# Average pooling 2x2x2: eight loads of 16 to 48 KB rows through one ring, and a store held back by an added wait

## The chip, the cores and the metric

One core of a Trainium2 chip. The metric is the device time of one execution in microseconds (us), lower is better. All runs told of here are fast (the full clock was granted). Times quoted are medians. A ratio is the mean time of one kernel's fast runs over that of the kernel before's fast runs of the same rounds, so it is not quite the ratio of the two medians.

## The reference, cut to what matters

```python
# x: (8, 32, 32, 32, 32) float32, kernel_size = 2; result: (8, 32, 16, 16, 16)
window = x[:, :, 2*i:2*i+2, 2*j:2*j+2, 2*k:2*k+2]
result[:, :, i, j, k] = np.mean(window, axis=(-3, -2, -1))
```

33.55 MB are read and 4.19 MB written, with seven additions and one product per result: a kernel about moving data. The 256 pairs of batch and channel lie on the 128 partitions in two halves (`t` = 0 and 1), each with rows of 128 KB. A "32 KB row" below is the piece of such a row that a load brings to each partition; its result is one eighth of it.

## The kernel before

```python
KF = 256                                    # 256 floats: 1 KB of a row
pool_in = ctx.enter_context(tc.tile_pool(name="pin", bufs=5))      # five buffers of 32 KB per partition
obuf = [pool_out.tile([P, 16 * KF], F32, name=f"obuf{t}") for t in range(2)]

plan = [(0, 0, (32,)), (0, 32, (32,)), (0, 64, (32,)), (0, 96, (32,)),
        (1, 0, (32,)), (1, 32, (32,)), (1, 64, (16, 16)), (1, 96, (16, 16))]

def pool_unit(buf, t, k0, kb):              # three Vector steps, in place in the loaded buffer
    nc.vector.tensor_add(out=b..., in0=a[:, :, 0], in1=a[:, :, 1])          # depth
    nc.vector.tensor_add(out=c, in0=bv[:, :, 0], in1=bv[:, :, 1])           # width
    nc.vector.tensor_tensor_reduce(out=obuf[t]..., scale=0.125, ...)        # height, times 1/8

for t, k0, parts in plan:
    tin = pool_in.tile([P, 32 * KF], F32, tag="tin", name="tin")
    ...                                     # one load per part on the Sync queue, then pool_unit on each

for t, k0, kb in [(1, 0, 12), (0, 0, 16), (1, 12, 4)]:    # three stores, on the same queue
    nc.sync.dma_start(out=ov[...], in_=obuf[t][:, k0 * KF:(k0 + kb) * KF])
# ... (after compiling: the first load is moved ahead of the opening barrier, and the
#      waits for the stores to the very end)
```

All transfers are issued by the Sync engine. It issues in program order, so a store that must wait for the Vector engine holds up everything behind it: in the run "the wait raised by four counts" below, the results of the 12 KB store were ready at 78.3 us, but it was issued at 82.89, right after the held 16 KB store.

Of the kernel before, what the change touches and what calls it, by code (L numbers as in the profile page):

```python
# [1 line left out]

# [4 lines left out]

F32 = mybir.dt.float32
KF = 256


@with_exitstack
def pool_rows(
    ctx: ExitStack,
    tc: tile.TileContext,
    x: bass.AP,
    kernel_size: int,
    out: bass.AP,
):
    nc = tc.nc  # L20
    assert kernel_size == 2, "only kernel_size == 2 supported"

    B, C, D, H, W = x.shape
    P = nc.NUM_PARTITIONS
    assert (B * C, D, H, W) == (2 * P, 32, 32, 32)
    add = mybir.AluOpType.add



    xv = x.rearrange("b c d h w -> (b c) (d h w)")  # L30
    ov = out.rearrange("b c d h w -> (b c) (d h w)")




    pool_in = ctx.enter_context(tc.tile_pool(name="pin", bufs=5))
    pool_out = ctx.enter_context(tc.tile_pool(name="pout", bufs=1))
    obuf = [pool_out.tile([P, 16 * KF], F32, name=f"obuf{t}") for t in range(2)]
    dummy = pool_out.tile([P, 1], F32, name="dummy")


    plan = [
        (0, 0, (32,)),
        (0, 32, (32,)),
        (0, 64, (32,)),
        (0, 96, (32,)),
        (1, 0, (32,)),
        (1, 32, (32,)),
        (1, 64, (16, 16)),
        (1, 96, (16, 16)),  # L50
    ]

    def pool_unit(buf, t, k0, kb):

        od = kb // 8
        a = buf.rearrange("p (o dd e) -> p o dd e", o=od, dd=2)
        b = buf[:, :od * 1024]
        nc.vector.tensor_add(  # L58
            out=b.rearrange("p (o e) -> p o e", o=od), in0=a[:, :, 0], in1=a[:, :, 1])
        bv = b.rearrange("p (e ww) -> p e ww", ww=2)  # L60
        c = buf[:, od * 1024:od * 1536]
        nc.vector.tensor_add(out=c, in0=bv[:, :, 0], in1=bv[:, :, 1])  # L62
        cv = c.rearrange("p (j hh k) -> p j hh k", hh=2, k=16)
        o0 = k0 * KF // 8
        nc.vector.tensor_tensor_reduce(  # L65
            out=obuf[t][:, o0:o0 + od * 256].rearrange("p (j k) -> p j k", k=16),
            in0=cv[:, :, 0], in1=cv[:, :, 1],
            scale=0.125, scalar=0.0, op0=add, op1=add, accum_out=dummy[:, :],
        )

    for t, k0, parts in plan:
        tin = pool_in.tile([P, 32 * KF], F32, tag="tin", name="tin")
        views = []
        o = 0
        for kb in parts:
            v = tin[:, o * KF:(o + kb) * KF]
            nc.sync.dma_start(
                out=v, in_=xv[t * P:(t + 1) * P, (k0 + o) * KF:(k0 + o + kb) * KF])
            views.append((v, k0 + o, kb))
            o += kb  # L80
        for v, k, kb in views:
            pool_unit(v, t, k, kb)



    for t, k0, kb in [(1, 0, 12), (0, 0, 16), (1, 12, 4)]:
        nc.sync.dma_start(
            out=ov[t * P:(t + 1) * P, k0 * KF:(k0 + kb) * KF],
            in_=obuf[t][:, k0 * KF:(k0 + kb) * KF],
        )  # L90


def kernel(tc: tile.TileContext, x: bass.AP, kernel_size: int, out: bass.AP):
    nc = tc.nc
    pool_rows(tc, x, kernel_size, out)
    tc.close()
    tc.compile()  # L97
    blocks = nc.main_func.blocks



    opening, program = blocks[0].instructions, blocks[tc.starting_block_idx].instructions
    load = next(i for i in program if isinstance(i, mybir.InstDMACopy))
    assert load.engine == nc.sync.engine
    barrier = next(
        n for n, i in enumerate(opening)
        if i.engine == load.engine and isinstance(i, mybir.InstDrain))
    program.remove(load)
    opening.insert(barrier, load)




    closing = blocks[-1].instructions
    stores = [
        i for i in program
        if isinstance(i, mybir.InstDMACopy) and "out_" in i.outs[0].memref]
    kept = [u.id for i in stores for u in i.sync_info.on_update]
    final = next(
        i for i in closing  # L120
        if i.engine == nc.sync.engine and isinstance(i, mybir.InstDrain))
    waits = {w.id: w for w in final.sync_info.on_wait}
    closing[closing.index(final)] = mybir.InstDrain(
        name=final.name, engine=final.engine, ins=[], outs=[], is_reset_sema=False,
        sync_info=mybir.SyncInfo(
            on_wait=[w for n, w in waits.items() if n not in kept], on_update=[]))


    reset = next(
        n for n, i in enumerate(closing)  # L130
        if isinstance(i, mybir.InstDrain) and i.is_reset_sema)
    first, stop = closing[reset].reset_range_start, closing[reset].reset_range_stop
    assert isinstance(closing[reset + 1], mybir.InstISA)
    while len(closing) > reset:
        closing.pop()
    n = first
    while n < stop:
        m = n
        while m < stop and m not in kept:
            m += 1  # L140
        if m > n:
            closing.append(mybir.InstDrain(
                name=nc.get_next_instruction_name(), engine=nc.gpsimd.engine, ins=[], outs=[],
                is_reset_sema=True, reset_range_start=n, reset_range_stop=m))
            nc.gpsimd.sem_clear(range(n, m))
        n = m + 1
    for n in kept:
        w = waits[n]
        closing.append(mybir.InstEventSemaphore(
            name=nc.get_next_instruction_name(), engine=nc.sync.engine, ins=[], outs=[],  # L150
            sync_info=mybir.SyncInfo(
                on_wait=[w],
                on_update=[mybir.SyncUpdate(
                    sync_type="semaphore", id=n, ant_name=w.ant_name,
                    update_mode="sem-sub-imm", update_value=w.wait_value)])))


# [1 line left out]
_INS = ['x', 'kernel_size']  # L159
_OUTS = [((8, 32, 16, 16, 16), 'float32')]  # L160

_NUMBERS = {'kernel_size': 2}


# [26 lines left out]
```

## Time and profile before

| | kernel before |
|---|---|
| time, first three runs | 91.36 us (91.27 to 91.69) |
| span of the profiled execution (instructions only) | 86.3 us |
| Vector engine busy | 64.0 us |
| last completion of a store by the packet records | 89.45 us |
| loads, stores | 10 (six of 32 KB rows, four of 16 KB rows), 3 |

The span ends with the last instruction, not with the last byte: here the stores go on for 3 us beyond it. So the span isn't the time. A "unit" is the Vector work on one load; the eight or ten units are counted from 1. A load or store is "completed" when its last packet is done; the page counts it as landed some 0.4 us later (the last store before: 85.14 + 4.7 = 89.8 us, last packet at 89.45). On a profile page each engine has a row of 40 digits, one for each fortieth of the span: the digit is the busy share in tenths (9 is 90% or more). Besides the page and its views, the text uses the trace's records of single DMA packets. One packet is one row of one partition; each of 16 engines carries 8 rows of a transfer and then a small completion packet. "Completion on the slowest engine" is the last of the 16.

### The profile page before, as it was taken

To read this page: it belongs to the slowest core of one execution; us is meant where nothing else is said; L and a number is where in the kernel's file an instruction comes from. 1 tells how busy PE (TensorE), PEld (TensorE's weight loads), DVE (VectorE), ACT (ScalarE), POOL (GpSimd) and SP (SyncE) were. 2 spreads that over 40 slices of the span, in tenths; PEclk is the share of its full clock that TensorE was granted. 3 is DMA by queue.
4 is the path that set the end of the run, shared out by engine and by line. 5 is a ranking of instruction groups with operands and counts; after the bars stand their busy time and mean duration, and the time that the engine had idled before them with its cause. 6 is when DMAs were issued, how large, how long until landed. Compare 5 with 4: busy or idle time off the path is not lost.

```text
span 86.3 us, 89 instructions
## 1 busy us (share of the span) xinstructions
DVE 64.0 (74%) x40; POOL 0.2 (0%) x4
## 2 busy tenths in 40 slices
DVE  0000049992999749992999749992999999999994
POOL 0000000000000000000000000000000000000000
DMA  8989997999969998899979998899999999999999
GB/s 243 395 380 441 486 486 334 395 486 486 486 289 441 486 486 380 349 486 486 486 304 425 486 486 380 365 471 387 463 387 463 387 463 395 456 425 412 433 431 441
DMA packets 1674, 36.60 MB, mean 424 GB/s; under 512 B 176, under 2 KB 176, under 8 KB 176
## 3 DMA queue, kind: packets, MB, share of 16 engines
q1 hardware_dynamic: 1674, 36.60, 99.4%
HBM read 33.55 MB, written 4.19 MB: 438 GB/s over the span
## 4 chain that ended last, share of the span: by engine, by line
DMA 61%; DVE 37%; issue 0%; DVEq 0%
DMA tin<-in_x_dram 61%; DVE tin L58 21%; DVE tin L62 11%; DVE obuf L65 6%; DVE dummy L65 0%; DVEq L97 0%
## 5 line engine op out<-in xcount | busy, mean ns | idle before, releaser
L58 DVE TENSOR_TENSOR tin<-tin 128x4096 f32<-128x4096 f32 (+1 forms) x10 | 35.7, 3569 | 20.5 <-DMA tin<-in_x_dram 20.5
L62 DVE TENSOR_TENSOR tin<-tin 128x2048 f32<-128x2048 f32 (+1 forms) x10 | 18.6, 1865 | 0.3
L65 DVE CUSTOM_DVE_ANT_1 obuf<-tin 128x1024 f32<-128x1024 f32 (+1 forms) x10 | 10.1, 1011 | 0.3
L65 DVE DVE_READ_ACCUMULATOR2_ANT dummy<- 128x1 f32 x10 | 0.8, 82 | 0.0
L172 POOL MEMSET const-bfloat16-1.0<- 128x1 bf16 x1 | 0.1, 102 | 0.0
L172 POOL MEMSET const-uint8-127<- 128x1 uint8 x1 | 0.1, 101 | 0.0
L172 POOL MEMSET const-float32-0.0<- 128x1 f32 x1 | 0.1, 99 | 0.2 <-issue 0.2
L172 POOL MEMSET const-float32-1.0<- 128x1 f32 x1 | 0.1, 98 | 0.0
## 6 DMA issues: line engine op xcount, KB each, us to landing
tin<-in_x_dram SPq DMA_DIRECT2D x6, 4096.0 KB, 34.8
tin<-in_x_dram SPq DMA_DIRECT2D x4, 2048.0 KB, 38.0
out_dram<-obuf SPq DMA_DIRECT2D x1, 2048.0 KB, 11.5
out_dram<-obuf SPq DMA_DIRECT2D x1, 1536.0 KB, 7.0
out_dram<-obuf SPq DMA_DIRECT2D x1, 512.0 KB, 4.7
```

The source lines that it names most:

```text
L58: nc.vector.tensor_add(out=b.rearrange("p (o e) -> p o e", o=od), in0=a[:, :, 0], in1=a[:, :, 1])
L62: nc.vector.tensor_add(out=c, in0=bv[:, :, 0], in1=bv[:, :, 1])
L65: nc.vector.tensor_tensor_reduce(out=obuf[t][:, o0:o0 + od * 256].rearrange("p (j k) -> p j k", k=16), in0=cv[:, :, 0], in1=cv[:, :, 1], s ...
L172: nc = _bacc.Bacc("TRN2", target_bir_lowering=False, num_devices=1)
```

## The change

The intent: the same 160 KB of buffer as one ring, cut so that fewer and longer loads fit; and a store of finished results first, held back until shortly before the other store is ready.

```diff
-    pool_in = ctx.enter_context(tc.tile_pool(name="pin", bufs=5))
+    ring = pool.tile([P, 160 * KF], F32, name="ring")
-    plan = [(0, 0, (32,)), (0, 32, (32,)), (0, 64, (32,)), (0, 96, (32,)),
-            (1, 0, (32,)), (1, 32, (32,)), (1, 64, (16, 16)), (1, 96, (16, 16))]
+    plan = [        # half, start, KB, place in the ring
+        (0, 0, 32, 0), (0, 32, 48, 32), (0, 80, 48, 80), (1, 0, 32, 128),
+        (1, 32, 32, 0), (1, 64, 32, 32), (1, 96, 16, 64), (1, 112, 16, 80)]
+        tc.keep_in_program_order(first)             # the first add of each unit
-    for t, k0, kb in [(1, 0, 12), (0, 0, 16), (1, 12, 4)]:
+    for t, k0, kb in [(0, 0, 16), (1, 0, 12), (1, 12, 4)]:
+    # the first store waits for the Vector counter that the second needs, less one
+    (n, store), (_, second) = stores[:2]
+    need, = [w for w in second.sync_info.on_wait if w.ant_name.startswith("DVE")]
+            w = copy.replace(w, wait_value=need.wait_value - 1)
+    program[n] = copy.replace(store, sync_info=mybir.SyncInfo(on_wait=waits, ...))
 ... (cut)
```

More of the change, by code (lines that the diff above doesn't have):

```diff
@@ L1 @@
+import copy
 from contextlib import ExitStack
@@ L31, in pool_rows @@
     ov = out.rearrange("b c d h w -> (b c) (d h w)")
-    pool_in = ctx.enter_context(tc.tile_pool(name="pin", bufs=5))
-    pool_out = ctx.enter_context(tc.tile_pool(name="pout", bufs=1))
-    obuf = [pool_out.tile([P, 16 * KF], F32, name=f"obuf{t}") for t in range(2)]
-    dummy = pool_out.tile([P, 1], F32, name="dummy")
+    pool = ctx.enter_context(tc.tile_pool(name="ring", bufs=1))
+    ring = pool.tile([P, 160 * KF], F32, name="ring")
+    obuf = [pool.tile([P, 16 * KF], F32, name=f"obuf{t}") for t in range(2)]
+    dummy = pool.tile([P, 1], F32, name="dummy")
     plan = [
-        (0, 0, (32,)),
-        (0, 32, (32,)),
-        (0, 64, (32,)),
-        (0, 96, (32,)),
-        (1, 0, (32,)),
-        (1, 32, (32,)),
-        (1, 64, (16, 16)),
-        (1, 96, (16, 16)),
+        (0, 0, 32, 0),
+        (0, 32, 48, 32),
+        (0, 80, 48, 80),
+        (1, 0, 32, 128),
+        (1, 32, 32, 0),
+        (1, 64, 32, 32),
+        (1, 96, 16, 64),
+        (1, 112, 16, 80),
     ]
@@ L57, in pool_unit @@
         b = buf[:, :od * 1024]
-        nc.vector.tensor_add(
+        first = nc.vector.tensor_add(
             out=b.rearrange("p (o e) -> p o e", o=od), in0=a[:, :, 0], in1=a[:, :, 1])
+        tc.keep_in_program_order(first)
         bv = b.rearrange("p (e ww) -> p e ww", ww=2)
@@ L69, in pool_unit @@
         )
-    for t, k0, parts in plan:
-        tin = pool_in.tile([P, 32 * KF], F32, tag="tin", name="tin")
-        views = []
-        o = 0
-        for kb in parts:
-            v = tin[:, o * KF:(o + kb) * KF]
-            nc.sync.dma_start(
-                out=v, in_=xv[t * P:(t + 1) * P, (k0 + o) * KF:(k0 + o + kb) * KF])
-            views.append((v, k0 + o, kb))
-            o += kb
-        for v, k, kb in views:
-            pool_unit(v, t, k, kb)
-    for t, k0, kb in [(1, 0, 12), (0, 0, 16), (1, 12, 4)]:
+    for t, k0, kb, r0 in plan:
+        unit = ring[:, r0 * KF:(r0 + kb) * KF]
+        nc.sync.dma_start(out=unit, in_=xv[t * P:(t + 1) * P, k0 * KF:(k0 + kb) * KF])
+        pool_unit(unit, t, k0, kb)
+    for t, k0, kb in [(0, 0, 16), (1, 0, 12), (1, 12, 4)]:
         nc.sync.dma_start(
@@ L98 @@
     blocks = nc.main_func.blocks
-    opening, program = blocks[0].instructions, blocks[tc.starting_block_idx].instructions
+    program = blocks[tc.starting_block_idx].instructions
+    stores = [
+        (n, i) for n, i in enumerate(program)
+        if isinstance(i, mybir.InstDMACopy) and "out_" in i.outs[0].memref]
+    (n, store), (_, second) = stores[:2]
+    need, = [w for w in second.sync_info.on_wait if w.ant_name.startswith("DVE")]
+    waits = []
+    for w in store.sync_info.on_wait:
+        if w.ant_name.startswith("DVE"):
+            assert w.id == need.id and w.wait_value < need.wait_value - 1
+            w = copy.replace(w, wait_value=need.wait_value - 1)
+        waits.append(w)
+    program[n] = copy.replace(store, sync_info=mybir.SyncInfo(
+        on_wait=waits, on_update=store.sync_info.on_update))
+    opening = blocks[0].instructions
     load = next(i for i in program if isinstance(i, mybir.InstDMACopy))
```

## The prediction

> **What bounds the kernel now.** I read the page first (busy shares, the 40 slices, the DMA queue), then the timeline of the Vector engine, then the waits of the DMA-issuing queue, then the trace's records of single DMA packets. The page, parts 1 to 3:
>
> ```profile
> DVE 64.0 (74%) x40; POOL 0.2 (0%) x4
> ...
> DVE  0000049992999749992999749992999999999994
> ...
> DMA  8989997999969998899979998899999999999999
> ...
> q1 hardware_dynamic: 1674, 36.60, 99.4%
> ```
>
> The reader is to see that the one queue keeps its 16 engines at work for 99.4% of the span, while the Vector engine has gaps up to slice 27 and is full after it. The chain of waits in part 4 puts 61% on loads and 37% on Vector work, but that chain ends with the last Vector instruction at 85.1 us. It doesn't see the three stores, which are still moving then. The end is set by the bytes. The timeline of the Vector engine gives the pace of the loads:
>
> ```profile
> 11.98 4.42 DVE L58 TENSOR_TENSOR tin<-tin 128x4096 f32<-128x4096 f32 x1 [11.98 <-DMA tin<-in_x_dram]
> ...
> 21.69 4.43 DVE L58 TENSOR_TENSOR tin<-tin 128x4096 f32<-128x4096 f32 x1 [1.69 <-DMA tin<-in_x_dram]
> ...
> 50.85 4.42 DVE L58 TENSOR_TENSOR tin<-tin 128x4096 f32<-128x4096 f32 x1 [1.71 <-DMA tin<-in_x_dram]
> ...
> 60.55 4.43 DVE L58 TENSOR_TENSOR tin<-tin 128x4096 f32<-128x4096 f32 x1 [1.68 <-DMA tin<-in_x_dram]
> ...
> 85.02 0.08 DVE L65 DVE_READ_ACCUMULATOR2_ANT dummy<- 128x1 f32 x1
> ```
>
> Each of the first six units starts when its load lands, 9.70 to 9.73 us after the one before: 4.194 MB in 9.71 us is 432 GB/s. The packet records say the same more finely. A row of 32 KB takes an engine 1.213 us, one of 16 KB 0.611 us; rows follow each other without a hole on every engine from the first packet at 1.02 us to the last store packet at 89.45 us. The completions of the slowest engine stand at 11.62, then 9.68 to 9.72 us apart for loads of 32 KB rows, 4.89 to 4.94 us for 16 KB rows (last load at 79.68), and for the stores 3.66 us (12 KB rows), 4.86 us (16 KB) and 1.25 us (4 KB), which ends at 89.45 us. The measured 91.25 us of the profiled run is this plus 1.8 us. So the bound is one unbroken DMA stream of 37.75 MB; the Vector engine matters only where it releases a transfer too late for the stream.
>
> It has slack everywhere but perhaps at the end. By the DMA issues, loads land a median of 34.8 us (32 KB rows) and 38.0 us (16 KB rows) after issue: several others are queued ahead of each. The last store is issued at 85.14 us, and the stream reaches it only at 87.8 us: 2.7 us of slack.
>
> **What the Trainium skill says.** "DMA: Bandwidth & Descriptors", section "Where 436 GB/s comes from", puts the ceiling of 16 SBUF ports at 435.2 GB/s and holds about 358 for the HBM side. The trace agrees with the first (432) and not with the second, as this core runs alone. The same page, section "Queues, rings and completion order", has descriptors of a ring consumed in order on each engine: the completions above, in the order of issue, agree. Its section "Latency and other measured facts" gives about 600 ns to the first byte of a DMA issued from Sync; in this trace the first load is issued at 0.0 and its first packets start at 1.02 to 1.64 us, so I use 1.0 to 1.6. "VectorE: DVE Perf Modes", section "Mode 1× (REGULAR) — the baseline", has one result per cycle for fp32 tensor_tensor; at that page's 0.96 GHz 4096 results are 4.27 us, and the trace has 4.43 with the fixed part.
>
> **The change part by part.** *Loads.* Ten loads become eight, with the same 33.55 MB. The cost of one load beyond its bytes: two loads of 16 KB rows take 2 x 4.89 = 9.78 us, one of 32 KB rows 9.69, so 0.09 us per load. Two fewer save 0.18 us of the stream. A load of 48 KB rows is then 9.69 + (9.69 - 4.89) = 14.49 us. The stream's completions on the slowest engine: 11.62; 26.11; 40.60; 50.29; 59.98; 69.67; 74.56; 79.45 us (before 79.68). Vector instructions start 0.36 us after such a completion (11.62 to 11.98).
>
> *Vector work.* Same elements. Two fewer units save two sets of fixed costs, and the program order is now kept, where before the first add of the sixth unit's follower slipped ahead. Start to start, a unit of 32 KB rows takes 7.94 us (11.98 to 19.92) and one of 16 KB rows 4.20 (76.63 to 80.83), so 3.74 us per further 16 KB: a 48 KB unit is 11.68 us. With the landings above:
> unit 1: 11.98 to 19.92; unit 2 (48): 26.47 to 38.15; unit 3 (48): 40.96 to 52.64; unit 4, landed 50.65, waits for the engine: 52.64 to 60.57; unit 5 (landed 60.34): to 68.51; unit 6: 70.03 to 77.97; unit 7 (landed 74.92): to 82.17; unit 8: to 86.36, and with the last accumulator read 86.45 us. That is 1.3 us later than the 85.1 of before: a 48 KB load leaves the engine idle until 26.47, and the two large units at the start are worked off late.
>
> *Ring.* Same 160 KB. The fifth load needs unit 1 gone (20.0), the sixth and seventh unit 2 (38.2), the eighth unit 3 (52.7). At those times the stream still has loads queued to 50.3, 60.0 and 74.6 us. Nothing starves.
>
> *Stores.* Before, the 12 KB store goes first at 76.74 and the 16 KB one follows at 77.13, ahead of the end of the loads at 79.68. After, the 16 KB store could have gone at 52.7; the added wait holds it until the counter of the Vector engine is one below what the 12 KB store needs. Each unit raises it three times (two adds, accumulator read), so it goes after the second add of unit 6: 70.03 + 4.46 + 2.33 = 76.8 us. With 1.0 to 1.6 us to the first packet it is at the engines at 77.8 to 78.4, before 79.45: no hole. The 12 KB store goes at 78.1, in time. Together they take 8.52 us, until 87.97 on the slowest engine and some 0.4 us earlier on the fastest (the spread of the completions of one transfer). The 4 KB store is released at 86.47 and is at the engines at 87.5 to 88.1: the slack of 2.7 us shrinks to somewhere between +0.5 and -0.1.
>
> *Sum.* Stream: -0.18 us for two loads fewer (the two schedules differ by 0.23, as one of the loads of before took 4.94). Hole before the last store: 0 to +0.3. The start, the tail after the last landing and the closing resets are not touched. Net between -0.2 and +0.1; from 91.36 I take 91.25 us.
>
> **The rivals.** (1) *The Vector engine becomes the bound at the end.* For it: my schedule puts its end at 86.45, 1.3 us later, and the last store has to pay its start-up after that. Were the latency of the last store 2.5 us rather than 1.0 to 1.6, the stream would stand still for about 1 us and the time would be about 92.2. Against it: even so it is under 1%, and the first load, on a cold queue, reached most engines by 1.3 us. (2) *The larger loads shorten the stream by more than I reckon*, as if a fixed time of every transfer lay bare. For it: every load costs something. Against it: the loads follow at 432 GB/s with packets end to end, and the 0.09 us per load is measured; the time could reach 91.1 and hardly less. (3) *The held-back store matters*: if its wait were met too late the stream would stop between loads and stores. It would have to be released after 78.4 us; my figure is 76.8, the same as the 76.74 of the first store before. If unit 6 came 1 us later the hole would be under 1 us. (4) *A store overtakes or mixes with loads.* The stream holds the same bytes at about the same rate for loads and stores, so mixing moves the time only by delaying the last loads, thus units 7 and 8; the added wait keeps the first store behind all loads in any case.
>
> **Range and chances.** The centre is 91.25 us. Run to run, before has 91.27 to 91.69, so 0.2 us either way is noise. Below, the two saved loads and luck give 90.95; above, a hole of 0.4 us before the last store and noise give 91.75. For a change over 2% (1.83 us) the stream would have to lose or win some 19 times 0.09 us, or the last store be late by nearly 2 us: nothing in the profile offers that. Faster by over 2%: 1%; within 2%: 97%; slower: 2%.
>
> **What would show each step.** In the profile of the changed kernel the second unit should start at about 26.5 us and the third at about 41.0 (48 KB load 14.5 us); unit 4 should wait for no DMA; the longest add over 6144 elements should be about 6.57 us; the last Vector instruction should end at about 86.4 and the span be about 87.6 us, longer than before by 1.3 although the time isn't. The 16 KB store should be issued at about 76.8 and the last at about 86.5, with only 2.7 to 3.3 us to landing rather than 4.7. The DMA share should stay at 99%. I would be wrong if 48 KB rows were moved at another rate, if the Vector engine slowed while both run, if packets of the last store started over 2 us after its issue, or if a hole stood between the last load and the first store.

## The result

| | before | changed |
|---|---|---|
| time, 6 runs each on one chip | 91.41 us (91.27 to 91.69) | 91.28 us (91.16 to 91.46) |
| ratio, 95% interval | | 0.9982 (0.9959 to 1.0004) |
| the changed kernel again, 5 runs beside 9 of before | 91.33 us | 91.20 us, ratio 0.9985 (0.9972 to 0.9997) |
| span | 86.3 us | 88.0 us |
| Vector busy, last Vector instruction ends | 64.0, 85.1 us | 63.2, 86.8 us |
| last completion of a load, of a store (slowest engine) | 79.68, 89.45 us | 79.72, 89.48 us |

Within 2%, as predicted, with the time predicted at 91.25. The gain of 0.13 to 0.16 us is clear of noise only in the second comparison. From the page of the changed kernel, busy shares, slices and the DMA queue:

```profile
DVE 63.2 (72%) x32; POOL 0.2 (0%) x4
...
DVE  0000049991008999942999999999999299999994
...
DMA  8979999888998889986999988999989999999999
...
q1 hardware_dynamic: 1440, 37.26, 99.1%
```

The queue stays full (99.1% against 99.4%) with fewer packets. The Vector engine's idle time has moved: the digits of slices 11 and 12 (counted from 1) are 0 where the first 48 KB load is awaited, and what it would have done there it does later. From the timeline of the changed kernel (start and duration in us, engine, line, operation, shapes, and in brackets the idle time and what ended it):

```profile
26.65 6.56 DVE L60 TENSOR_TENSOR ring<-ring 128x6144 f32<-128x6144 f32 x1 [6.49 <-DMA ring<-in_x_dram]
...
41.21 6.56 DVE L60 TENSOR_TENSOR ring<-ring 128x6144 f32<-128x6144 f32 x1 [2.81 <-DMA ring<-in_x_dram]
...
52.88 4.42 DVE L60 TENSOR_TENSOR ring<-ring 128x4096 f32<-128x4096 f32 x1
...
77.15 10.00 SPq L81 DMA_DIRECT2D out_dram<-obuf  x3
...
86.70 0.08 DVE L68 DVE_READ_ACCUMULATOR2_ANT dummy<- 128x1 f32 x1
```

The two large units start 14.56 us apart; the fourth waits for no DMA; the stores are issued from 77.15 us on, and the last Vector instruction is 1.7 us later than before. The issues of the three stores (size in KB, us from issue to landing) in the changed kernel:

```profile
out_dram<-obuf SPq DMA_DIRECT2D x1, 2048.0 KB, 7.9
out_dram<-obuf SPq DMA_DIRECT2D x1, 1536.0 KB, 10.2
out_dram<-obuf SPq DMA_DIRECT2D x1, 512.0 KB, 3.1
```

And of the last store in the kernel before:

```profile
out_dram<-obuf SPq DMA_DIRECT2D x1, 512.0 KB, 4.7
```

The last store landed 4.7 us after its issue in the kernel before and 3.1 us here: it is issued 1.7 us later (86.81 against 85.14) and lands at the same time, having waited less in the queue.

### The profile page after: what moved, and what is told of

Read it like the earlier page. It is cut to its first block, busy times and chain, and to the rows that moved or that the text cites. A ratio compares the mean times of both kernels' runs of the same rounds, so it can differ in the third digit from the quotient of the medians.

```text
span 88.0 us, 78 instructions
## 1 busy us (share of the span) xinstructions
DVE 63.2 (72%) x32; POOL 0.2 (0%) x4
## 3 DMA queue, kind: packets, MB, share of 16 engines
q1 hardware_dynamic: 1440, 37.26, 99.1%
## 4 chain that ended last, share of the span: by engine, by line
DMA 66%; DVE 32%; issue 0%; DVEq 0%
DMA ring<-in_x_dram 66%; DVE ring L60 18%; DVE ring L65 9%; DVE obuf L68 5%; DVE dummy L68 0%; DVEq L91 0%
## 5 line engine op out<-in xcount | busy, mean ns | idle before, releaser
L60 DVE TENSOR_TENSOR ring<-ring 128x4096 f32<-128x4096 f32 (+2 forms) x8 | 35.4, 4422 | 23.0 <-DMA ring<-in_x_dram 23.0
L65 DVE TENSOR_TENSOR ring<-ring 128x2048 f32<-128x2048 f32 (+2 forms) x8 | 18.3, 2292 | 0.3
L68 DVE CUSTOM_DVE_ANT_1 obuf<-ring 128x1024 f32<-128x1024 f32 (+2 forms) x8 | 9.8, 1225 | 0.3
```

Source lines behind the costliest of these rows:

```text
L60: first = nc.vector.tensor_add(out=b.rearrange("p (o e) -> p o e", o=od), in0=a[:, :, 0], in1=a[:, :, 1])
L68: nc.vector.tensor_tensor_reduce(out=obuf[t][:, o0:o0 + od * 256].rearrange("p (j k) -> p j k", k=16), in0=cv[:, :, 0], in1=cv[:, :, 1], s ...
```

## The experiments

Twelve runs were made, eleven of them of new kernels, all with correct results. The first four were to settle which part of the change does what; they brought a surprise, and the next four went after it; the last four test the sizes that the prediction rests on. The kernel before ran beside them, with medians of 91.34, 91.33 and 91.37 us in the three groups of four.

### Without the added wait

```diff
-    program[n] = copy.replace(store, sync_info=mybir.SyncInfo(
-        on_wait=waits, on_update=store.sync_info.on_update))
```

> The changed kernel without the added wait: the 16 KB store is free to be issued at 52.9 us, as soon as units 1 to 3 are worked off. One stream in order of issue (my theory): it lies behind the eighth load, issued at 51.5 us, so its packets still start at 79.3 to 79.7 us and nothing moves; time 91.3 us, within 0.2 of the changed kernel, issue to landing of that store about 32 us instead of 7.9. Rival, stores mix with or overtake queued loads: the last loads land up to 4.9 us later, the last Vector instruction ends after 88 us, and the time is 92.5 to 94 us.

Measured: 92.10 us (91.81 to 92.22), ratio 1.0066 (1.0041 to 1.0092); some 0.8 us over the changed kernel. The store was issued at 52.92 us and landed 33.0 us later. It did stay behind the loads: by the packet records its rows start at 80.2 us. But the loads ahead of it were late: the last one completes at 80.71 us, not 79.72. Neither theory had this. The throughput by stretch shows where it happened. First the changed kernel, then this one (stretch, length, busy time of Vector and GpSimd with instructions, clock, DMA share, GB/s; a packet counts whole in the stretch in which it starts, so in short stretches the share can pass 1 and the GB/s are rough):

```profile
70.00:76.50 6.50, 6.10 (x2) 0.00 (x0) 1.00 1.01 431
76.50:79.00 2.50, 2.47 (x4) 0.00 (x0) 1.00 1.02 439
79.00:82.00 3.00, 2.93 (x3) 0.00 (x0) 1.00 1.00 426
```

```profile
70.00:76.50 6.50, 6.19 (x2) 0.00 (x0) 1.00 1.03 436
76.50:79.00 2.50, 2.47 (x4) 0.00 (x0) 1.00 0.93 236
79.00:82.00 3.00, 2.93 (x3) 0.00 (x0) 1.00 1.01 431
```

In the stretch from 76.5 to 79.0 us the engines are as busy as ever (share 0.93) but move 236 GB/s instead of 439. By the packets, two rows of 16 KB on each engine, starting at about 76.9 and 78.0 us, take 1.0 to 1.2 us instead of 0.61; the two load rows after them take 0.61 again, and only then do the store's rows start. The time lost is not paid back later: from the last load's completion to the last store's it is 9.77 us here and 9.76 in the changed kernel. So with this order of the stores the added wait is worth more than the rest of the change gains: it keeps a store out of the queue while those loads run.

### The wait raised by four counts

```diff
-            w = copy.replace(w, wait_value=need.wait_value - 1)
+            w = copy.replace(w, wait_value=need.wait_value + 3)
```

> The same wait four counts later: the first store is held until unit 7 is worked off, at 82.6 us, while the loads end at 79.3 to 79.7 us. My theory (an empty stream needs 1.0 to 1.6 us from issue to first packet): first store packets at 83.6 to 84.2 us, a hole of about 4.2 us on each engine, all three stores shifted by it, time 95.3 us (95.0 to 95.8). Rival, that the stores have hidden slack and the end is set by the Vector engine's last instruction and the last store alone: time within 1 us of the changed kernel.

Measured: 95.21 us, ratio 1.0412. Its throughput by stretch:

```profile
76.00:79.00 3.00, 2.97 (x4) 0.00 (x0) 1.00 1.02 437
79.00:82.00 3.00, 2.93 (x3) 0.00 (x0) 1.00 0.00 0
82.00:83.50 1.50, 1.50 (x3) 0.00 (x0) 1.00 0.41 175
```

The stream runs dry, and the time follows it nearly one for one (holes of 3.8 to 4.3 us, 3.9 us more): the end is set by the bytes in the queue. The store was issued at 82.50 us and the first packets of the 16 engines start at 83.34 to 83.49: an empty queue costs 0.84 to 0.99 us here, less than the 1.0 to 1.6 that I had taken from the first load.

### The loads alone

```diff
-    for t, k0, kb in [(0, 0, 16), (1, 0, 12), (1, 12, 4)]:
+    for t, k0, kb in [(1, 0, 12), (0, 0, 16), (1, 12, 4)]:
 ... (and the added wait taken out)
```

> The new ring and the eight loads alone; the stores in the old order 12, 16, 4 KB with no added wait. The 12 KB store can go only after unit 6, at 78.4 us, 1.2 us later than the first store of the changed kernel, so its packets start at 79.4 to 80.0 against an end of the loads at 79.3 to 79.7: a hole of 0.1 to 0.4 us. My theory: 91.3 to 91.7 us, some 0.1 to 0.4 over the changed kernel. Rival, that the order of the stores and the wait do nothing: equal to the changed kernel, 91.3 us.

Measured: 91.16 us (91.06 to 91.25), ratio 0.9968 (0.9946 to 0.9990). Better than either expectation, and not to be told from the changed kernel's second run (91.11 to 91.25). The 12 KB store went at 78.39 us; with 0.86 us of latency its first rows start at 79.25 and the loads end at 79.20 to 79.65 us. The hole I reckoned with isn't there, as I had taken the latency too long. The gain of the change thus comes with the loads alone; the new order of the stores and the wait add nothing that can be measured.

### The stores alone

The loads and buffers of the kernel before, with the new order of stores and the added wait (edits of the change section).

> The loads and buffers of the kernel before with the new order of the stores (16, 12, 4 KB) and the added wait. My theory: the stream has the ten loads of before and never a hole, so the time is that of before, 91.4 us, within 0.15, and the 0.1 to 0.2 us of the changed kernel come from its loads. Rival, that the order of the stores gives the gain: 91.25 us, equal to the changed kernel.

Measured: 92.05 us (91.74 to 92.12), ratio 1.0055 (1.0028 to 1.0082): slower, against both expectations. With the units of before the same wait is met at 76.11 us, and the rows of the last load from 77.3 us on are slow. The throughput of this kernel in the same stretch:

```profile
76.50:79.00 2.50, 2.50 (x3) 0.00 (x0) 1.00 0.99 341
```

and of the kernel before:

```profile
76.50:79.00 2.50, 2.46 (x4) 0.00 (x0) 1.00 1.02 433
```

So the same order and wait that do no harm beside the new loads do harm beside the old ones; the store is released 1 us earlier here.

### The wait lowered by one count

```diff
-            w = copy.replace(w, wait_value=need.wait_value - 1)
+            w = copy.replace(w, wait_value=need.wait_value - 2)
```

> The changed kernel with the added wait one count lower: the 16 KB store is released after the first add of unit 6, at about 74.8 us instead of 77.15. Theory from the run without the wait: rows of loads that an engine starts while a store's rows already lie behind them in its queue are slowed, the last two from 0.61 to about 1.1 us each. The store is at the engines at 75.8, before the last two rows (76.9 and 78.0) start, so the last load is late by about 1.0 us and the time 92.0 to 92.2 us. Rival, that the slow rows have another cause, for instance the very long wait in the queue (25 us) of the run without the wait: 91.3 us, like the changed kernel.

Measured: 91.97 us (91.89 to 92.13), ratio 1.0071 (1.0058 to 1.0085). The store was issued at 74.73 us, and the slow stretch is back:

```profile
76.50:79.00 2.50, 2.47 (x4) 0.00 (x0) 1.00 1.01 295
```

A store that has lain in the queue for 2 us does much the same harm (0.8 us on an engine by the packets, against 0.95) as one that has lain there for 24, at nearly the same place of the load. The rival falls.

### The stores of before in the new order, released at the old time

```diff
-            w = copy.replace(w, wait_value=need.wait_value - 1)     # of "the stores alone"
+            w = copy.replace(w, wait_value=need.wait_value)
```

> The kernel before with its stores in the order 16, 12, 4 KB, but the first held until unit 7 of its ten is worked off, at 76.8 us, as late as the first store of before (76.74); the earlier run of this order had it at 76.11 and lost 0.7 us. If the time of issue decides: 91.2 to 91.6 us, like before. If it is the order, or the 16 KB rows of the first store: 92.0 us again.

(By the timeline it is the eighth of the ten units, not the seventh, that ends at 76.8 us; the time is what was meant.)

Measured: 91.36 us (91.31 to 91.46), ratio 1.0004 (0.9991 to 1.0016). The 16 KB store went at 76.80 us, 0.7 us later than in "the stores alone", and the loss is gone:

```profile
76.50:79.00 2.50, 2.47 (x3) 0.00 (x0) 1.00 1.06 452
```

Neither the order of the stores nor the rows of the first one matters here; its time does.

### The changed kernel again

No edit.

> The changed kernel unaltered, a second time, on the chip of these runs: 91.3 us (91.15 to 91.5), ratio to before 0.997 to 1.000, no slowed rows at the end of the loads. If the 0.13 us of the first comparison were chance, the ratio would be 1.000 or above.

Measured: 91.20 us (91.11 to 91.25), ratio 0.9985 (0.9972 to 0.9997). The store went at 77.06 us, no load row at the end was slow. The small gain is confirmed.

### Without the wait, the last load in two of 8 KB rows

```diff
-        (1, 112, 16, 80),
+        (1, 112, 8, 80),
+        (1, 120, 8, 88),
```
(and the added wait taken out)

> As the run without the wait, but the last load of 16 KB rows is two loads of 8 KB rows; the 16 KB store lies behind them from 53 us on. If a fixed number of rows is slowed in proportion to their size, the two last rows of 8 KB lose about 0.25 us each: time 91.7 us. If each of the last two rows loses a fixed 0.5 us, or if a fixed number of bytes (32 KB, now four rows) is slowed: about 1.0 us lost, 92.2 us; the packets then tell which, two rows of about 0.8 us or four rows of about 0.55 us instead of 0.31.

Measured: 91.99 us (91.79 to 92.05), ratio 1.0069 (1.0056 to 1.0081), between the two figures. The packets decide: on most engines two to four rows of 8 KB, starting at about 76.9 to 78.6 us, take 0.4 to 0.66 us instead of 0.31, then nearly all rows are at 0.31 to 0.38 again. The last load is 0.8 us late. So it is not a fixed number of rows but nearly the same stretch of time; whether time or bytes decide (16 to 32 KB on an engine here, 32 KB in the run without the wait), the two runs don't tell.

### Rows cut into pieces of 8 KB, with the same ten loads

```diff
+G = 8 * KF + 8                              # 8 KB and a gap of 32 bytes
-        tin = pool_in.tile([P, 32 * KF], F32, tag="tin", name="tin")
+        tin = pool_in.tile([P, 4 * G], F32, tag="tin", name="tin")
-                out=v, in_=xv[...])
+                out=v.rearrange("p (o g) -> p o g", g=G)[:, :, :8 * KF],
+                in_=xv[...].rearrange("p (o g) -> p o g", g=8 * KF))
```
(from the kernel before; the first add reads past the gaps)

> The kernel before with its ten loads, but each row cut into pieces of 8 KB by a gap of 32 bytes in the buffer: 256 packets per engine for the loads instead of 80, the same number of transfers and semaphores. If what a load costs beyond its bytes (0.09 us in the prediction, 8 rows per engine, so 11 ns per packet) is a cost per packet: 176 packets more per engine, up to 2.0 us, time 93.3 us. If it is a cost per transfer (its completion): 91.4 us, like before. The 8 KB rows seen in an earlier run took 0.307 us each, against 0.303 us per 8 KB in rows of 32 KB; by that it is 0.7 us, time 92.0 us.

Measured: 92.93 us, ratio 1.0168 (1.0148 to 1.0188). The timeline shows the loads of 32 KB rows landing 9.86 to 9.96 us apart, where the kernel before has 9.70 to 9.73. Three of the six:

```profile
22.37 4.43 DVE L60 TENSOR_TENSOR tin<-tin 128x4096 f32<-128x4096 f32 x1 [1.94 <-DMA tin<-in_x_dram]
...
32.25 4.42 DVE L60 TENSOR_TENSOR tin<-tin 128x4096 f32<-128x4096 f32 x1 [1.86 <-DMA tin<-in_x_dram]
...
42.11 4.42 DVE L60 TENSOR_TENSOR tin<-tin 128x4096 f32<-128x4096 f32 x1 [1.85 <-DMA tin<-in_x_dram]
```

The median difference is 1.56 us for 176 packets more on each engine: 8.9 ns per packet on average. Of it 0.44 us fall on the first load (unit 1 starts at 12.42 us, not 11.98); between the later loads it is (9.916 - 9.714) / 24 = 8.4 ns. The gaps in the buffer are not the cause: the rows of 8 KB take 0.312 us here and in the next run, which has no gaps (medians).

### 32 loads of 8 KB rows

```diff
-            nc.sync.dma_start(
-                out=v, in_=xv[...])
+            for q in range(0, kb, 8):
+                nc.sync.dma_start(
+                    out=v[:, q * KF:(q + 8) * KF], in_=xv[...])
```
(from the kernel before)

> The kernel before with each load cut into loads of 8 KB rows: 32 transfers instead of 10, Vector work unchanged. If each load costs 0.09 us beyond its bytes, as the prediction has it: 22 x 0.09 = 2.0 us more, 93.3 us. If the loads of 8 KB rows seen in an earlier run (2.45 us each, so 9.80 instead of 9.69 for 32 KB) tell it: 0.7 us more, 92.0 us. Against the run with the rows cut but the transfers kept, the difference is the cost of a transfer's completion alone.

Measured: 93.23 us, ratio 1.0211 (1.0188 to 1.0233). The DMA issues of this kernel:

```profile
tin<-in_x_dram SPq DMA_DIRECT2D x32, 1024.0 KB, 19.9
```

The difference is 1.86 us for 22 loads more: 0.085 us each, where the prediction had 0.09. Most of it is the packets: the run above has the same number of load rows in ten transfers and costs 1.56 us, so the transfer itself costs (1.86 - 1.56) / 22 = 0.014 us, an estimate from the small difference of two runs.

### The last two loads as one of 32 KB rows

```diff
-        (1, 96, 16, 64),
-        (1, 112, 16, 80),
+        (1, 96, 32, 64),
```

> The changed kernel with its last two loads of 16 KB rows as one of 32 KB rows: one load fewer, but the last unit lands at 80.0 and ends at 88.0 us instead of 86.8. If the changed kernel's last store has just no slack left and needs 0.95 us from issue to first packet (as measured for the store held to 82.5 us): packets at 89.1 us against a stream that is dry at 87.6 to 88.1, so the stream ends 1.0 to 1.2 us later: 92.2 to 92.5 us. If the last store had slack of over 1 us: 91.2 us.

Measured: 92.13 us (92.03 to 92.24), ratio 1.0081. The last store was issued at 88.02 us and its first packets start at 88.85 to 89.00 us, while the engines had been without work from 87.7 to 88.1 us on. The throughput by stretch:

```profile
83.50:87.00 3.50, 3.43 (x3) 0.00 (x0) 1.00 1.01 432
87.00:88.70 1.70, 0.99 (x2) 0.00 (x0) 1.00 0.36 152
```

A last Vector instruction 1.2 us later than in the changed kernel costs 0.9 us. So the changed kernel's last store does have almost no slack left: 0.3 us at most. Its own trace agrees: its first row starts at 87.80 us, 0.99 us after the issue at 86.81.

### The 16 KB store ahead of the last load

```diff
+        if n == len(plan) - 1:
+            nc.sync.dma_start(out=ov[0:P, 0:16 * KF], in_=obuf[0][:, :])
-    for t, k0, kb in [(0, 0, 16), (1, 0, 12), (1, 12, 4)]:
+    for t, k0, kb in [(1, 0, 12), (1, 12, 4)]:
```
(from the changed kernel, the added wait taken out)

> The changed kernel without the wait, with the 16 KB store issued before the last load, not after it. If every load that has a store's rows behind it in the queue loses 1.0 us: the seventh load loses it before the 16 KB store and the eighth before the 12 KB store; the eighth lands at 80.0 + 4.9 + 2.0 = 86.9, its unit ends at 91.1, and the last store is at the engines at 92.0 while the stream has been dry since 90.3 us; end at 93.3, time 95 us (94.6 to 95.4). If the loss belongs to the end of all loads alone, or is paid once: 94 us. If stores inside the loads cost nothing beyond the delay of the last unit: 92.8 to 93.1 us.

Measured: 94.40 us, ratio 1.0331. The last unit started at 86.09 us:

```profile
86.09 2.29 DVE L60 TENSOR_TENSOR ring<-ring 128x2048 f32<-128x2048 f32 x1 [3.58 <-DMA ring<-in_x_dram]
```

The seventh load, with the 16 KB store behind it, again had two rows of 0.8 to 1.3 us on most engines, at 72.5 to 74 us, and completed at 75.67 instead of 74.7: the loss isn't bound to the end of all loads. But the eighth load, with the 12 KB store behind it from 78.34 us, 6 us ahead of its end, had only single rows of 0.7 to 0.9 us and lost 0.2 us or so; the time is nearest to the 94 us of "paid once". "Every load with a store behind it loses 1 us" is refuted by that.

### What the experiments say together of the release of the first store

The loads end at 79.1 to 79.8 us (first to last engine) in all these kernels when nothing slows them.

| run | first store, issued at | loads | ratio to before |
|---|---|---|---|
| without the wait | 16 KB, 52.92 us | 8 | 1.0066 |
| wait lowered by one | 16 KB, 74.73 us | 8 | 1.0071 |
| stores alone | 16 KB, 76.11 us | 10 | 1.0055 |
| before | 12 KB, 76.74 us | 10 | 1 |
| new order at the old time | 16 KB, 76.80 us | 10 | 1.0004 |
| changed | 16 KB, 77.15 and 77.06 us | 8 | 0.9982, 0.9985 |
| loads alone | 12 KB, 78.39 us | 8 | 0.9968 |
| wait raised by four | 16 KB, 82.50 us | 8 | 1.0412 |

Within a release from 76.7 to 78.4 us, that is 2.5 to 0.8 us before the fastest engine is done with its loads, nothing is lost. In the three runs with an earlier release 0.5 to 0.8 us are; in the one with a later release, by 4.1 us, 3.9 us are. Within the window the times order by the loads: ten at 1, eight at 0.997 to 0.9985.

What stays open is the mechanism of the slow rows. That an engine begins to read a queued store's rows while the loads' rows ahead of them are still being written would fit the place of the slow stretch, but the records give no reads by themselves, the time isn't paid back later, and the eighth load of the last run above hardly suffers. That is a guess, not shown. Open too is whether some executions of the kernel before meet the same thing: its packets show two slow rows at most (0.72 us) at 78.3 us and its store goes at the early edge of the window, and 7 of its 37 runs took 91.66 to 91.86 us, where no run of the changed kernel took over 91.46. It would fit, but none of those executions has a trace, and of the five whose span is on record two had 86.8 us instead of 86.3 to 86.4, which slow rows at the end don't bring about ("stores alone" kept 86.4). If it holds, it is a part of the ratio's gain. It isn't all of it: from the first load's completion to the end of the last store (means of the 16 engines) the traces have 77.81 and 77.81 us with ten loads (before, new order at the old time) and 77.73, 77.66 and 77.73 with eight (changed, again, loads alone), all without more than two slow rows of a load.

No version beats the changed kernel clearly. "Loads alone" is its equal in simpler code.

## Why the prediction was right, point by point

- *The bound is one unbroken DMA stream.* Right. The stream dry for some us (wait raised by four, last two loads as one) costs about what the hole is long.
- *Two loads fewer save 0.18 us.* Right in size: 0.085 us per load in the run with 22 loads more, nearly all of it a cost of packets. With the measured parts it is 16 packets fewer per engine x 8.9 ns + 2 x 0.014 = 0.17 us; the two comparisons have 0.13 us between the medians. In the one profiled execution it can't be seen in the end, since there the first load landed 0.16 us later than in before.
- *The schedule of the Vector engine.* Right within 0.4 us, of which 0.16 is that late first landing: unit 2 at 26.65 us (26.47), unit 3 at 41.21 (40.96), unit 4 without a DMA wait, the end at 86.8 (86.45), the add over 6144 elements 6.56 us (6.57). The span grew by 1.7 us (1.3) and the time did not.
- *The ring starves nowhere.* Right; the queue's share is 99.1%, and no engine has a gap of over 0.06 us between two packets. (The eighth load could go at 51.19 us, after the second add of unit 3, not at 52.7; nothing hung on it.)
- *The last store keeps +0.5 to -0.1 us of slack.* Right, and on the good side: the latency term was oversized. It was taken from the first load (1.0 to 1.6 us); the stores that met an empty queue have 0.83 to 1.0 us. This is why "hole before the last store: 0 to +0.3" came out as 0.
- *The held-back store.* The number was right (77.15 us against 76.8, no hole). The reason was not seen: the third rival feared only a wait met too late, and the fourth held that mixing "moves the time only by delaying the last loads", with loads and stores at the same rate. The runs show that a store in the queue too early slows loads ahead of it by up to 1 us. The sum stayed right since the added wait, and in before the wait for results, both kept the first store out of that time. Here the prediction was lucky: it held for a reason that it did not give. From the same argument dropping the wait was expected to cost nothing; it cost 0.8 us.
- *A slip:* 1.83 us is 20 times 0.09 us, not 19. Nothing rests on it.

## What to carry to other kernels

When one queue is full from start to end, reckon the change in packets and transfers, and check each release against the moment at which the queue would run dry; a span or a Vector engine that ends later need not cost anything. Where long loads are still queued ahead of a store whose data are ready, try a later release. In this kernel the good time was about 0.8 to 2.5 us before the loads end, and 0.6 us decided (76.11 against 76.74 us); the window elsewhere is not known, so take it from a trace. When a wait seems to hold back work that is ready, take it out in a run before calling it waste.

## What the Trainium skill lacked or had wrong

- No page tells that a queued store slows loads ahead of it in the same queue. Measured: rows of 16 KB at 1.0 to 1.2 us instead of 0.61 for about 2 us, 439 to 236 GB/s in the same stretch of two runs, 0.5 to 0.8 us of the time. It would belong to "DMA: Bandwidth & Descriptors", section "Queues, rings and completion order".
- "DMA: Bandwidth & Descriptors", section "Latency and other measured facts": about 600 ns to the first byte from the Sync queue, without saying from which moment it counts. The runs have 0.83 to 1.0 us from the start of the issuing instruction to the first packet of a store on an empty queue; that instruction takes 0.33 to 0.35 us, so from its end it is 0.50 to 0.66 us, which agrees. For the first load of the program it is 1.0 to 2.1 us from the start.
- No page has a figure for what one more transfer costs in a queue that is full. Measured for loads from Sync: 0.014 us beyond its packets, an estimate from two runs. It would belong to the same page.
- The same page, section "Where 436 GB/s comes from", says that the HBM side (about 358 GB/s) binds a transfer between HBM and SBUF. That sentence is too broad for a core that runs alone: this one had 432 GB/s. (The page says elsewhere that 358 is the share of a core when both cores of a pair stream.)
